# A two-block RWKV / state-space kernel: small products padded to the full array, two heads in turn, fewer changes of array shape

## The chip, the cores and the metric

One core of a Trainium2 chip runs the whole program as one launch. The metric is the device time of that launch in microseconds. Each program was timed in several runs; the median counts. A profile is one further execution, with a span (first to last instruction) and its own time.

## The reference

One sequence of 256 positions, width 2048, float32, through two blocks. The first block has an RWKV-7 time mix (16 heads of 64), a sparse attention with a learned index (16 heads), gates, and a product-key feed-forward with 16384 experts. The second block has a Mamba-2 mixer (64 heads of 64, state 128, 8 groups) and a sliding-window attention. Three parts matter here:

```
# RWKV, per head, for every position t
sa = S @ (-kk_t);  S = S * w_t + sa (kk_t a_t)^T + v_t k_t^T;  y_t = S @ r_t
w_log = -softplus(-(w0 + tanh(zw) @ w_decay_up)) - 0.5
a = sigmoid(a0 + za @ w_icl_up);  g = sigmoid(zg) @ w_gate_up
# Mamba-2, chunks of 128
y_diag = einsum("bgcqs,bgrcqs,bcsgrp->bcqgrp", C B^T, decay_in, x)
y_off  = einsum("bcqgn,bcgrpn,bgrcq->bcqgrp", C, start_states, exp(da_cum))
```

## The kernel before

Large projections run in `K.gemm` (lines 204 and 206): weights come in as float32, ScalarE rounds them to a high part `hi`, VectorE subtracts to get `lo`, and TensorE adds `x*hi` (512 columns) and `x*lo` (256 columns) into one of six large PSUM banks named `g`. The small products work on float32 operands and take one of two small PSUM banks that `k.bank(name)` hands out in turn: `psS`, `psY`, `psQ`, `psA`, `psy` are names of such banks. In the trace a float32 product is two matmul records, here called passes; a transpose or a `g` product is one.

**RWKV** (`Rwkv.pair`, eight pairs of heads, three pairs in flight through `weave`, while a projection's `g` products are put in between by the framework's scheduler). Head 0 of a pair lies on partitions 0 to 63, head 1 on 64 to 127, time is cut in four chunks of 64 (`tt`, `cc`). What the change touches:

- `psA` (lines 464 to 466): the low-rank products for `a` and the gate `g`, with 64, 128 and 32 rows of the array in use.
- `psS` (line 550): the products between chunk vectors, 64 rows each, all four of head 0 into one bank, then all four of head 1 into the other. Five VectorE instructions (lines 554 to 556) read each bank.
- `psQ` (line 642): the state that enters a chunk, times `At`, 64 of 128 output columns in use, three times per pair.
- `psY` (lines 662 and 664): the output. Per chunk two 64-column products (one for each head) and, where a state enters, one of full shape.

**Mamba** (`Mamba.group`, eight groups, as the side generator of a projection). Per half of a group (four heads, `hh`), two units `u` each fill a bank `psy`: four products with 64 output columns that need the decay matrix `M` (line 1528), then two full ones that don't (lines 1530, 1533), then the reads.

In the notation of the trace, 64\*128 is 64 rows by 128 columns of the array in use. A matmul's instruction carries an array shape: 128\*128 (full), 64\*128 and 32\*128 (rows only in part) or 128\*64 (columns only in part).

Of the kernel before, what the change touches and what calls it, by code (L numbers as in the profile page):

```python
# [14 lines left out]
AF = mybir.ActivationFunctionType  # L15
ALU = mybir.AluOpType
# [4 lines left out]
T = 256  # L21
# [351 lines left out]
class Rwkv:  # L373
# [56 lines left out]
    def lora(self):  # L430
        k, nc, pool = self.k, self.k.nc, self.pool
        th = self.th = pool.tile([65, T], F32, name="th")
        nc.vector.memset(th[64:65, :], 1.0)
        nc.scalar.activation(th[0:64, :], self.z[24][0:64, :], AF.Tanh)
        self.za = self.z[24]
        for z in (self.z[25], self.z[26][0:32]):
            k.sigmoid(z, z)

    WIDTH = 3

    def pair(self, hp):
        k, nc, pool, par, c = self.k, self.k.nc, self.pool, self.par, self.c
        f0 = hp * 128
        col = lambda n: par[n][:, hp:hp + 1]
        W = lambda n, shape, bufs=1, dt=F32, p=pool: p.tile(shape, dt, tag="w_" + n, bufs=bufs, name=n)
        L = lambda n, shape: W(n, shape, self.WIDTH)
        last = self.last
        V, S, P, E = nc.vector, nc.scalar, nc.gpsimd, nc.tensor
        halves = [slice(0, 64), slice(64, 128)]
        le, lt = c["leC"], c["ltC"]  # L450

        r, kr, v = (W(f"z{n}", [128, T]) for n in "rkv")
        for i, t in enumerate((r, kr, v)):
            nc.sync.dma_start(t, self.zd[8 * i + hp])
        wg = W("wg", [128, 2, 128])
        fs = slice(f0, f0 + 128)
        nc.scalar.dma_start(wg[:, 0, :], k.a["w_gate_up"][0, 0:128, fs])
        nc.scalar.dma_start(wg[0:32, 1, :], k.a["w_gate_up"][0, 128:160, fs])
        nc.scalar.dma_start(wg[64:128, 1, :], k.a["w_icl_up"][0, :, fs])
        wd = W("wd", [65, 128], 2)  # L460
        nc.scalar.dma_start(wd[0:64, :], k.a["w_decay_up"][0, :, fs])
        nc.scalar.dma_start(wd[64:65, :], k.a["w0"][:, fs])
        psA = k.bank("psA")
        E.matmul(psA[:, 0:T], lhsT=wg[64:128, 1, :], rhs=self.za[64:128, :], start=True, stop=True)
        E.matmul(psA[:, T:], lhsT=wg[:, 0, :], rhs=self.z[25], start=True, stop=False)
        E.matmul(psA[:, T:], lhsT=wg[0:32, 1, :], rhs=self.z[26][0:32, :], start=False, stop=True)
        av = W("a", [128, T])
        k.sigmoid(av, psA[:, 0:T], self.ha0[:, hp:hp + 1])
        g = L("g", [128, T])
        S.copy(g, psA[:, T:])  # L470
        ps = k.bank("psD")
# [8 lines left out]
        for tt in range(2):  # L480
            for i in range(2):
                E.matmul(psC[:, tt * 256:(tt + 1) * 256], lhsT=s2[:, i, tt * 128:(tt + 1) * 128], rhs=self.tri,
                         start=(i == 0), stop=(i == 1))
# [29 lines left out]
        Ah, Rh = AR[:, 0], AR[:, 1]  # L513
        BK = W("BK", [128, 2, 4, 64])
# [8 lines left out]
        two = lambda ap: ap.rearrange("p q t -> p (q t)")  # L523
# [3 lines left out]
        for tt in range(2):  # L527
            ps = k.bank("psR")
# [13 lines left out]
        MR = L("MR", [128, 2, 2, 2, 64])  # L542
        for i, hs in enumerate(halves):
            P.memset(LB[hs, :, halves[1 - i]], 0.0)
            P.memset(LK[hs, :, halves[i]], 0.0)
        for h in range(2):
            ps = k.bank("psS").rearrange("p (a c b t) -> p a c b t", a=2, c=2, b=2)
            for tt in range(2):
                for cc in range(2):
                    E.matmul(ps[:, tt, cc], lhsT=two(BK[halves[h], tt, 2 * cc:2 * cc + 2]),  # L550
                             rhs=AR[halves[h], :, tt, halves[cc]], start=True, stop=True)
            for i, hs in enumerate(halves):
                m = lt[hs, None, :].to_broadcast([64, 2, 64])
                V.tensor_tensor(LB[hs, 2 * h:2 * h + 2, hs], ps[hs, :, i, 0], m, op=ALU.mult)
                V.tensor_tensor(LK[hs, 2 * h:2 * h + 2, halves[1 - i]], ps[hs, :, 1 - i, 0], m, op=ALU.mult)
            V.tensor_tensor(MR[:, h], ps[:, :, :, 1], le[:, None, None, :].to_broadcast([128, 2, 2, 64]), op=ALU.mult)
            yield
        psX = k.bank("psX")
        for i in range(4):
            h, tt = divmod(i, 2)  # L560
            E.matmul(psX[:, i * 64:(i + 1) * 64], lhsT=LK[:, i, :], rhs=VS[:, tt, h], start=True, stop=True)
        S.copy(XA[:, :, 0], psX[:, 0:256].rearrange("p (h a v) -> p a h v", h=2, a=2))
        UV = W("UV", [128, 2, 2, 2, 64], 2)
# [10 lines left out]
        ps = k.bank("psT0")  # L574
# [6 lines left out]
        for lv in range(4):  # L581
            ps = k.bank("psU")
# [5 lines left out]
            ps = k.bank("psW")  # L588
# [4 lines left out]
            ps = k.bank("psV")  # L593
# [32 lines left out]
        ps = k.bank("psT1")  # L626
        for tt in range(2):
            E.transpose(ps[:, tt * 128:(tt + 1) * 128], XA[:, tt, 1].rearrange("p h d -> p (h d)"), k.ident)
        At = W("At", [128, 2, 128], 2)
# [3 lines left out]
        y = W("y", [128, T], 2, p=last)  # L633
        Sd = None
        for tt in range(2):
            starts = []
            for cc in range(2):
                cs = halves[cc]
                starts.append(Sd)
                if Sd is not None:  # L640
                    ps = k.bank("psQ")
                    E.matmul(ps[cs, 0:128], lhsT=At[:, tt, cs], rhs=Sd, start=True, stop=True)
                    u = UV[cs, tt, cc]
                    V.tensor_tensor(u, ps[cs, 0:128].rearrange("p (h v) -> p h v", h=2), u, op=ALU.add)
                    yield
                if tt == 1 and cc == 1:
                    break
                ps2 = k.bank("psZ")
                if Sd is not None:
                    E.matmul(ps2[:, 0:128], lhsT=k.ident, rhs=Sd, start=True, stop=False)  # L650
                E.matmul(ps2[:, 0:128], lhsT=ROW[:, tt, cc], rhs=two(UV[:, tt, cc]), start=(Sd is None), stop=True)
                Sn = W("St", [128, 128], 4, p=last)
                P.memset(Sn, 0.0)
                for h, hs in enumerate(halves):
                    S.activation(Sn[hs, hs], ps2[hs, hs], AF.Copy, scale=gC[hs, tt, cc:cc + 1])
                Sd = Sn
                yield
            psY = k.bank("psY")
            for cc, s in enumerate(starts):
                cs = halves[cc]  # L660
                for h, hs in enumerate(halves):
                    E.matmul(psY[hs, cs], lhsT=UV[:, tt, cc, h], rhs=MR[:, h, tt, cc], start=True, stop=(s is None))
                if s is not None:
                    E.matmul(psY[:, cs], lhsT=s, rhs=Rh[:, tt, cs], start=False, stop=True)
            S.copy(y[:, tt * 128:(tt + 1) * 128], psY[:, 0:128])
            yield

        psG = k.bank("psG")
# [706 lines left out]
class Mamba:  # L1375
# [93 lines left out]
    def group(self, g):  # L1469

        k, nc, pool, c = self.k, self.k.nc, self.pool, self.c
        V, S, P, E = nc.vector, nc.scalar, nc.gpsimd, nc.tensor
        W = lambda n, shape, bufs=2, dt=F32: pool.tile(shape, dt, tag="w_" + n, bufs=bufs, name=n)
        B, C = self.xs[32 + g], self.xs[40 + g]
        xs = self.xs[4 * g:4 * g + 4]
        h0 = 8 * g

        xd = W("xd", [128, 2, 8, 64])
        psb = k.bank("psb")
        for ch in range(2):  # L1480
            cs = slice(ch * 128, (ch + 1) * 128)
            ps = k.bank("psx")
# [23 lines left out]
        for hh in range(0, 8, 4):  # L1506
            M = []
            for ch in range(2):
                r4 = W("r4", [128, 2, 4, 128], dt=F32R)
                ps = k.bank("psg")  # L1510
                for i in range(4):
                    h = h0 + hh + i
                    S.activation(r4[:, 0, i], c["le"], AF.Copy, scale=self.dar[:, ch, h:h + 1])
                    (V if i % 2 else P).tensor_scalar(r4[:, 1, i], c["le"], self.dal[:, ch, h:h + 1], None, op0=ALU.mult)
                for i in range(2):
                    E.matmul(ps, lhsT=self.gt, rhs=r4[:, i].rearrange("p h t -> p (h t)"), start=(i == 0), stop=(i == 1))
                m = W("m", [128, 4, 128], 3)
                S.activation(m, ps.rearrange("p (h t) -> p h t", h=4), AF.Exp)
                V.tensor_tensor(m, m, cb[:, ch, None, :].to_broadcast([128, 4, 128]), op=ALU.mult)
                M.append(m)  # L1520
                yield
            for u in range(2):
                j = (hh + 2 * u) // 2
                hA = hh + 2 * u
                ps = k.bank("psy")
                for ch in range(2):
                    for e in range(2):
                        E.matmul(ps[64 * e:64 * e + 64, ch * 128:(ch + 1) * 128], lhsT=xd[:, ch, hA + e, :],
                                 rhs=M[ch][:, 2 * u + e, :], start=True, stop=True)
                E.matmul(ps[:, 256:384], lhsT=st[:, hA * 64:hA * 64 + 128], rhs=C[:, 128:256], start=True, stop=True)  # L1530
                db = W("db", [128, 2, 64])
                P.tensor_copy(db, self.dar[:, 1, h0 + hA:h0 + hA + 2, None].to_broadcast([128, 2, 64]))
                E.matmul(ps[:, 384:512], lhsT=db.rearrange("p e d -> p (e d)"), rhs=c["le"], start=True, stop=True)
                ec = W("ec", [128, 128])
                S.activation(ec, ps[:, 384:512], AF.Exp)
                V.tensor_tensor(ec, ps[:, 256:384], ec, op=ALU.mult)
                x = xs[j]
                V.scalar_tensor_tensor(x, x, self.dcol[:, 4 * g + j:4 * g + j + 1], ps[:, 0:T], op0=ALU.mult, op1=ALU.add)
                P.tensor_tensor(x[:, 128:256], x[:, 128:256], ec, op=ALU.add)
                yield  # L1540

# [525 lines left out]
```

## Time and profile before

| | |
|---|---|
| median of 3 runs | 3754.48 us (3749.0 to 3759.8) |
| the profiled execution's own time | 3757.85 us |
| its span | 3756.1 us |
| granted TensorE clock, mean | 0.992 |
| TensorE busy | 3634.1 us, 97% of the span |
| weight loads / VectorE / ScalarE / GpSimd busy | 80% / 71% / 53% / 35% |

The page's shares of busy time are averages over stages. A table by stretch tells which engine is full in a stage; the list of instructions in order of time gives the start of each group, and the distance between the start of one and of the next is what it costs in the stream. Durations of matmuls overlap and are modelled, so here only starts are compared. `x8` at the end of a row of that list means eight passes in a row.

### The profile page before, as it was taken

Reading aid. Unit: us, or ns where it says so; the run is one execution under the profiler, and the core shown is the slowest. Engines: PE = TensorE matmul, PEld = TensorE weight load, DVE = VectorE, ACT = ScalarE, POOL = GpSimd, SP = SyncE. Lnnn points to the kernel's source line nnn. Section 1 sums busy time; section 2 is a strip of 40 time slices with the busy share of each in tenths; the row PEclk is TensorE's granted clock in tenths of the full one; section 3 lists DMA queues with packets and bytes.
Section 4 is the critical chain, followed back from the end, with each engine's and each line's share of the span. In section 5 each row is a group of like instructions: output and inputs, shape, how many; then the busy total and the mean of one; then the engine's idle time right before and its main releaser. Section 6 shows DMA issues by size and latency. Waiting matters only on the chain.

```text
span 3756.1 us, 56311 instructions
## 1 busy us (share of the span) xinstructions
PE 3634.1 (97%) x19927; PEld 3023.4 (80%) x19927; DVE 2671.5 (71%) x4261; ACT 1985.7 (53%) x3739; POOL 1320.7 (35%) x1322
## 2 busy tenths in 40 slices
PE   9999999999999999998899999999999999989998
PEld 7778878878888888877788888887888887878777
DVE  5776767666688888888644444446899879577776
ACT  5445555545454677766444444445555666444553
POOL 1333223321288777655511111112144443151101
PEclk9999999999999999999999999999999999999999
DMA  7453433568598888878777766665544445545334
GB/s 219 125 165 113 130 107 110 169 225 254 166 204 207 199 212 222 210 180 207 232 236 239 239 231 231 223 197 182 180 151 146 153 134 165 184 150 185 124 113 136
DMA packets 358335, 681.24 MB, mean 181 GB/s; under 512 B 43981, under 2 KB 111477, under 8 KB 354853
## 3 DMA queue, kind: packets, MB, share of 16 engines
q1 hardware_dynamic: 305216, 591.50, 53.9%
q10 hardware_dynamic: 52837, 86.14, 6.9%
q8 instruction: 158, 2.59, 0.3%
q14 instruction: 124, 1.02, 0.1%
HBM read 627.57 MB, written 47.22 MB: 180 GB/s over the span
## 4 chain that ended last, share of the span: by engine, by line
PE 45%; DVE 8%; DMA 2%; issue 2%; ACT 2%; POOL 0%; ACTq 0%; DVEq 0%; SPq 0%; POOLq 0%
PE g L204 12%; PE g L206 6%; PE gv L1238 5%; PE gv L1237 5%; PE gv L1236 5%; DVE tr L1176 2%; PE dv L1236 2%; PE dv L1237 2%; PE dv L1238 2%; DVE lo L141 2%; DVE oh L1152 1%; ACT hi L139 1%; PE psl L1825 1%; PE g L228 1%; PE pso L1852 1%
## 5 line engine op out<-in xcount | busy, mean ns | idle before, releaser
L141 DVE TENSOR_TENSOR lo<-raw,hi 128x1024 fp32r<-128x1024 f32 (+3 forms) x856 | 1047.1, 1226 | 697.7 <-ACT hi L139 677.8
L139 ACT CAST hi<-raw 128x1024 fp32r<-128x1024 f32 (+3 forms) x858 | 867.5, 1014 | 979.7 <-PE g L204 345.4
L204 PE MATMUL g<-x,hi 128*128 128x512 f32 x3040 | 1089.3, 400 | 13.2 <-DVE x L1646 9.0
L206 PE MATMUL g<-x,lo 128*128 128x256 f32 x3040 | 842.8, 288 | 11.4 <-DVE lo L141 11.2
L1195 PE MATMUL gu<-x,hi 128*128 128x512 f32 x2048 | 733.7, 398 | 4.1 <-ACT hi L139 4.1
L141 POOL TENSOR_TENSOR lo<-tr,hi 128x512 fp32r<-128x512 f32 x429 | 591.5, 1408 | 262.0 <-ACT hi L139 182.3
L204 PEld LDWEIGHTS g<-x,hi 128*128 128x128 f32 x3040 | 568.2, 189 | 135.6 <-issue 19.6
L206 PEld LDWEIGHTS g<-x,lo 128*128 128x128 f32 x3040 | 574.6, 189 | 46.2 <-DVE lo L141 19.5
L1196 PE MATMUL gu<-x,lo 128*128 128x256 f32 x2048 | 581.6, 284 | 13.2 <-POOL lo L141 9.7
L1195 PEld LDWEIGHTS gu<-x,hi 128*128 128x128 f32 x2048 | 386.9, 189 | 91.1 <-ACT hi L139 5.4
L1196 PEld LDWEIGHTS gu<-x,lo 128*128 128x128 f32 x2048 | 387.7, 189 | 22.2 <-POOL lo L141 16.9
L1176 DVE STREAM_TRANSPOSE tr<-raw 128x1024 f32<-128x1024 f32 x256 | 309.1, 1231 | 88.9 <-POOL lo L141 47.8
L139 ACT CAST hi<-tr 128x512 fp32r<-128x512 f32 x512 | 289.4, 615 | 65.0 <-PE gu L1195 37.0
L141 POOL TENSOR_TENSOR g<-scr,g 128x512 fp32r<-128x512 f32 x64 | 112.2, 1754 | 574.4 <-ACT g L139 574.4
L1238 PE MATMUL gv<-hi,g 128*128 128x512 f32 x756 | 299.7, 396 | 0.0
L1237 PE MATMUL gv<-lo,g 128*128 128x512 f32 x756 | 299.7, 396 | 0.0
L1236 PE MATMUL gv<-hi,g 128*128 128x512 f32 x756 | 238.4, 396 | 0.0
L1204 ACT ACTIVATE act<-act 128x256 f32<-128x256 f32 x128 | 53.4, 417 | 242.2 <-DVE act L240 224.7
L204 PE MATMUL g<-y2m,hi 128*128 128x512 f32 x512 | 173.6, 395 | 0.0
L1238 PEld LDWEIGHTS gv<-hi,g 128*128 128x128 f32 x756 | 142.4, 188 | 34.7
L1237 PEld LDWEIGHTS gv<-lo,g 128*128 128x128 f32 x756 | 142.4, 188 | 34.7
L1236 PEld LDWEIGHTS gv<-hi,g 128*128 128x128 f32 x756 | 142.4, 188 | 34.7
(595 smaller groups left out, 5912.1 us busy)
## 6 DMA issues: line engine op xcount, KB each, us to landing
raw<-in_peer_u_dram SPq DMA_DIRECT2D x512, 256.0 KB
raw<-in_peer_v_dram SPq DMA_DIRECT2D x256, 512.0 KB
raw<-in_a_w_in_dram SPq DMA_DIRECT2D x160, 512.0 KB
raw<-in_w_in_dram SPq DMA_DIRECT2D x136, 512.0 KB
raw<-in_b_w_in_dram SPq DMA_DIRECT2D x64, 512.0 KB
raw<-in_a_w_out_dram SPq DMA_DIRECT2D x48, 512.0 KB
raw<-in_w_out_dram SPq DMA_DIRECT2D x32, 512.0 KB
raw<-in_w_peer_query_dram SPq DMA_DIRECT2D x32, 512.0 KB
```

The costliest lines, as they stand in the source:

```text
L139: ins = nc.scalar.copy(hi, x) if heng == "act" else nc.vector.tensor_copy(hi, x)
L141: return ins, eng.tensor_tensor(lo, x, hi.bitcast(F32), op=ALU.subtract)
L204: nc.tensor.matmul(ps[f], lhsT=hi[:, k, f * 128:(f + 1) * 128], rhs=x2[:, q, :], start=(q == 0), stop=False)
L206: nc.tensor.matmul(ps[f][:, 0:T], lhsT=lo[:, k, f * 128:(f + 1) * 128], rhs=x2[:, q, 0:T], start=False, stop=(q == nk - 1))
L228: nc.tensor.matmul(ps[tt], lhsT=x, rhs=lo[:, k, 0:n], start=False, stop=False)
L1176: st["t"] = nc.vector.transpose(tr.rearrange("p b (u j) -> p u b j", u=2), raw[:, 2 * u:2 * u + 2].rearrange("p u (b j) -> p u b j", j=32))
L1195: nc.tensor.matmul(ps, lhsT=hi[:, j], rhs=self.hn2[:, q, :], start=(q == 0), stop=False)
L1196: st["m"] = nc.tensor.matmul(ps[:, 0:T], lhsT=lo[:, j], rhs=self.hn2[:, q, 0:T], start=False, stop=(q == KT - 1))
L1204: nc.scalar.activation(o, o, AF.Gelu)
L1236: nc.tensor.matmul(p, lhsT=x, rhs=hi, start=first, stop=False)
L1237: nc.tensor.matmul(p, lhsT=x, rhs=lo, start=False, stop=False)
L1238: nc.tensor.matmul(p, lhsT=g2[:, T + tt * 128:T + tt * 128 + 128], rhs=hi, start=False, stop=last)
```

## The change

- **psA**: both low-rank operands are laid out over 128 partitions, with zeros written in the unused ones (three memsets on GpSimd once, one of 32 partitions per pair), so all three products use the full shape.
- **psS**: both heads' banks are taken at once, and the loops are turned so that the two heads come in turn.
- **psQ**: all 128 columns of `At` are used instead of 64; only the needed half is read.
- **psY**: the two 64-column products of a chunk become one of 128 columns by 128 columns of both heads; the state's product gets its 64 columns repeated for both heads; the off-diagonal quarters are never read. One ScalarE copy becomes two of half the partitions.
- **psy**: both units' banks are taken at once. The full products of both come first, then all eight 64-column ones, then the reads.

```diff
@@ Rwkv.lora
-        self.za = self.z[24]
         for z in (self.z[25], self.z[26][0:32]):
             k.sigmoid(z, z)
+        nc.gpsimd.memset(self.z[24][0:64], 0.0)
+        for r in (slice(32, 64), slice(64, 128)):
+            nc.gpsimd.memset(self.z[26][r], 0.0)
@@ Rwkv.pair
+        P.memset(wg[32:64, 1, :], 0.0)
...
-        E.matmul(psA[:, 0:T], lhsT=wg[64:128, 1, :], rhs=self.za[64:128, :], start=True, stop=True)
+        E.matmul(psA[:, 0:T], lhsT=wg[:, 1, :], rhs=self.z[24], start=True, stop=True)
         E.matmul(psA[:, T:], lhsT=wg[:, 0, :], rhs=self.z[25], start=True, stop=False)
-        E.matmul(psA[:, T:], lhsT=wg[0:32, 1, :], rhs=self.z[26][0:32, :], start=False, stop=True)
+        E.matmul(psA[:, T:], lhsT=wg[:, 1, :], rhs=self.z[26], start=False, stop=True)
...
-        for h in range(2):
-            ps = k.bank("psS").rearrange("p (a c b t) -> p a c b t", a=2, c=2, b=2)
-            for tt in range(2):
-                for cc in range(2):
-                    E.matmul(ps[:, tt, cc], lhsT=two(BK[halves[h], tt, 2 * cc:2 * cc + 2]),
+        both = [k.bank("psS").rearrange("p (a c b t) -> p a c b t", a=2, c=2, b=2) for _ in range(2)]
+        for tt in range(2):
+            for cc in range(2):
+                for h in range(2):
+                    E.matmul(both[h][:, tt, cc], lhsT=two(BK[halves[h], tt, 2 * cc:2 * cc + 2]),
                              rhs=AR[halves[h], :, tt, halves[cc]], start=True, stop=True)
+        for h, ps in enumerate(both):
...
-                    E.matmul(ps[cs, 0:128], lhsT=At[:, tt, cs], rhs=Sd, start=True, stop=True)
+                    E.matmul(ps[:, 0:128], lhsT=At[:, tt], rhs=Sd, start=True, stop=True)
...
-                for h, hs in enumerate(halves):
-                    E.matmul(psY[hs, cs], lhsT=UV[:, tt, cc, h], rhs=MR[:, h, tt, cc], start=True, stop=(s is None))
+                E.matmul(psY[:, cc], lhsT=two(UV[:, tt, cc]), rhs=MR[:, :, tt, cc], start=True, stop=(s is None))
                 if s is not None:
-                    E.matmul(psY[:, cs], lhsT=s, rhs=Rh[:, tt, cs], start=False, stop=True)
-            S.copy(y[:, tt * 128:(tt + 1) * 128], psY[:, 0:128])
+                    E.matmul(psY[:, cc], lhsT=s, rhs=Rh[:, tt, None, halves[cc]].to_broadcast([128, 2, 64]), start=False,
+                             stop=True)
+            for h, hs in enumerate(halves):
+                S.copy(y[hs, tt * 128:(tt + 1) * 128].rearrange("p (c t) -> p c t", c=2), psY[hs, 0:2, h])
@@ Mamba.group
+            ps = [k.bank("psy") for _ in range(2)]
+            for u in range(2):
+                hA = hh + 2 * u
+                db = W("db", [128, 2, 64])
+                P.tensor_copy(db, self.dar[:, 1, h0 + hA:h0 + hA + 2, None].to_broadcast([128, 2, 64]))
+                E.matmul(ps[u][:, 256:384], lhsT=st[:, hA * 64:hA * 64 + 128], rhs=C[:, 128:256], start=True, stop=True)
+                E.matmul(ps[u][:, 384:512], lhsT=db.rearrange("p e d -> p (e d)"), rhs=c["le"], start=True, stop=True)
+            for u in range(2):
+                for ch in range(2):
+                    for e in range(2):
+                        E.matmul(ps[u][64 * e:64 * e + 64, ch * 128:(ch + 1) * 128], lhsT=xd[:, ch, hh + 2 * u + e, :],
+                                 rhs=M[ch][:, 2 * u + e, :], start=True, stop=True)
```

The scheduler makes TensorE's order anew. In its order of instructions before, the array's shape changes 473 times; now, 305 times. Away from the two stages the order of TensorE is the same.

TensorE in the RWKV stage before, in the fourth pair (`psS_3391` is head 0's bank, `psS_3415` head 1's; `psY` and `psW` belong to the pairs ahead):

```order
L584 MATMUL psU_3377<-TT_3164,LB_3062 128x64 x4
L204 MATMUL g_5935<-o2b_89,hi_5941 128x512
L550 MATMUL psS_3391<-AR_3323,BK_3324 128x128 x4
L662 MATMUL psY_3401<-MR_2777,UV_2821 64x64 x2
L664 MATMUL psY_3401<-AR_2727,St_3275 128x64
L662 MATMUL psY_3401<-MR_2777,UV_2821 64x64 x2
L664 MATMUL psY_3401<-AR_2727,St_3354 128x64
L206 MATMUL g_5935<-o2b_89,lo_5942 128x256
L204 MATMUL g_5935<-o2b_89,hi_5941 128x512
L206 MATMUL g_5935<-o2b_89,lo_5942 128x256
L590 MATMUL psW_3409<-U_3382,Q_3156 128x64 x4
```

Head 1's four `psS` products stand three rows further down. Now, in the same place:

```order
L589 MATMUL psU_3381<-TT_3168,LB_3067 128x64 x4
L554 MATMUL psS_3395<-AR_3327,BK_3328 128x128 x3
L554 MATMUL psS_3396<-AR_3327,BK_3328 128x128 x3
L554 MATMUL psS_3395<-AR_3327,BK_3328 128x128
L554 MATMUL psS_3396<-AR_3327,BK_3328 128x128
L206 MATMUL g_5929<-o2b_89,lo_5957 128x256
L204 MATMUL g_5929<-o2b_89,hi_5956 128x512
L206 MATMUL g_5929<-o2b_89,lo_5957 128x256
```

Both heads stand together, in turn; then nine `g` products (three are shown), then `psY`, now four products of 128x128. Of the eight pairs six have `psS` in one visit to the shape that had two, the first had one already, and one pair still has two.

TensorE in the Mamba stage before, one half of a group (`psy_26154` and `psy_26168` are the two units):

```order
L1528 MATMUL psy_26154<-m_26116,xd_26034 64x128 x2
L1528 MATMUL psy_26168<-m_26116,xd_26034 64x128 x2
L1528 MATMUL psy_26154<-m_26131,xd_26034 64x128 x2
L1530 MATMUL psy_26154<-xs41_25113,st_26079 128x128
L1533 MATMUL psy_26154<-const_ssd_24312,db_26160 128x128
L1528 MATMUL psy_26168<-m_26131,xd_26034 64x128 x2
L1530 MATMUL psy_26168<-xs41_25113,st_26079 128x128
L1533 MATMUL psy_26168<-const_ssd_24312,db_26174 128x128
```

And now, the end of the same half (the four full products stand ahead, among `g` products):

```order
L204 MATMUL g_26352<-x2_78,hi_26651 128x512
L1538 MATMUL psy_26149<-m_26111,xd_26029 64x128 x2
L1538 MATMUL psy_26150<-m_26111,xd_26029 64x128 x2
L1538 MATMUL psy_26149<-m_26126,xd_26029 64x128 x2
L1538 MATMUL psy_26150<-m_26126,xd_26029 64x128 x2
L206 MATMUL g_26352<-x2_78,lo_26652 128x256
```

Two visits to the 64-column shape became one here. Over the sixteen halves the visits for `psy` fall from 46 to 28.

## Rows read from the trace of the kernel before

**Rows 1.** The page, busy time by engine.

```profile
PE 3634.1 (97%) x19927; PEld 3023.4 (80%) x19927; DVE 2671.5 (71%) x4261; ACT 1985.7 (53%) x3739; POOL 1320.7 (35%) x1322
```

**Rows 2.** Busy us by stretch: RWKV, Mamba; length, engines, clock, DMA share, GB/s.

```profile
240.00:720.00 480.00, 464.50 (x2959) 387.53 (x2958) 342.43 (x656) 259.79 (x543) 142.06 (x225) 0.99 0.39 123
2700.00:3080.00 380.00, 380.00 (x2291) 317.85 (x2290) 323.71 (x590) 222.75 (x445) 167.65 (x225) 1.00 0.46 147
```

**Rows 3.** PE in order of time around one psQ; start us, length us, engine, line.

```profile
419.14 0.39 PE L204 MATMUL g<-o2b,hi 128*128 128x512 f32 x1
419.37 0.28 PE L206 MATMUL g<-o2b,lo 128*128 128x256 f32 x1
419.49 0.40 PE L204 MATMUL g<-o2b,hi 128*128 128x512 f32 x1
419.82 0.43 PE L642 MATMUL psQ<-St,At 128*64 128x128 f32 x2
420.18 0.39 PE L206 MATMUL g<-o2b,lo 128*128 128x256 f32 x1
420.41 0.39 PE L204 MATMUL g<-o2b,hi 128*128 128x512 f32 x1
```

**Rows 4.** The same view, the fourth pair's psS, then psY and psW.

```profile
421.57 0.47 PE L204 MATMUL g<-o2b,hi 128*128 128x512 f32 x1
421.97 1.16 PE L550 MATMUL psS<-AR,BK 64*128 64x128 f32 x8
423.06 0.34 PE L662 MATMUL psY<-MR,UV 128*64 128x64 f32 x4
423.32 0.43 PE L664 MATMUL psY<-AR,St 128*128 128x64 f32 x2
...
424.20 0.37 PE L206 MATMUL g<-o2b,lo 128*128 128x256 f32 x1
...
424.75 1.10 PE L590 MATMUL psW<-U,Q 128*128 128x64 f32 x8
425.66 0.48 PE L204 MATMUL g<-o2b,hi 128*128 128x512 f32 x1
```

**Rows 5.** The same view, the first pair, where both heads' psS ran together.

```profile
274.97 1.72 PE L550 MATMUL psS<-AR,BK 64*128 64x128 f32 x16 [0.15 <-ACT VS L535]
276.62 0.50 PE L204 MATMUL g<-x,hi 128*128 128x512 f32 x1
```

**Rows 6.** The same view, psA of one pair.

```profile
445.80 0.70 PE L464 MATMUL psA<-z,wg 64*128 64x256 f32 x2
...
447.68 0.71 PE L473 MATMUL psD<-wd,th 65*128 65x128 f32 x4
```

**Rows 7.** The same view, full-shape passes of 256 columns.

```profile
101.72 1.03 PE L748 MATMUL psN<-csq,const_f 128*128 128x256 f32 x4
102.39 0.58 PE L204 MATMUL g<-x,hi 128*128 128x512 f32 x1
```

**Rows 8.** The same view: psy in the Mamba stage, twelve passes together, four alone.

```profile
2775.05 0.88 PE L1528 MATMUL psy<-m,xd 128*64 128x128 f32 x12
2775.86 0.49 PE L1530 MATMUL psy<-xs,st 128*128 128x128 f32 x2
...
2970.08 0.28 PE L206 MATMUL g<-x,lo 128*128 128x256 f32 x1
2970.29 0.44 PE L1528 MATMUL psy<-m,xd 128*64 128x128 f32 x4
2970.66 0.49 PE L204 MATMUL g<-x,hi 128*128 128x512 f32 x1
```

**Rows 9.** By line: a copy, a memset, the longest read of psS; ns min/median/max, start us.

```profile
L665 ACT COPY y<-psY x16: 265/265/266, 352.6 to 700.5; 128x128 f32<-128x128 f32 x16
...
L545 POOL MEMSET M<- x16: 304/306/309, 236.1 to 597.1; 64x256 f32 x16
...
L556 DVE TENSOR_TENSOR MR<-psS,const_rw x16: 423/425/427, 277.2 to 645.3; 128x256 f32<-128x256 f32 x16
```

More of the change, by code (lines that the diff above doesn't have):

```diff
@@ L657, in pair @@
                 yield
-            psY = k.bank("psY")
+            psY = k.bank("psY").rearrange("p (c h t) -> p c h t", c=4, h=2)
             for cc, s in enumerate(starts):
-                cs = halves[cc]
-                for h, hs in enumerate(halves):
-                    E.matmul(psY[hs, cs], lhsT=UV[:, tt, cc, h], rhs=MR[:, h, tt, cc], start=True, stop=(s is None))
+                E.matmul(psY[:, cc], lhsT=two(UV[:, tt, cc]), rhs=MR[:, :, tt, cc], start=True, stop=(s is None))
                 if s is not None:
-                    E.matmul(psY[:, cs], lhsT=s, rhs=Rh[:, tt, cs], start=False, stop=True)
-            S.copy(y[:, tt * 128:(tt + 1) * 128], psY[:, 0:128])
+                    E.matmul(psY[:, cc], lhsT=s, rhs=Rh[:, tt, None, halves[cc]].to_broadcast([128, 2, 64]), start=False,
+                             stop=True)
+            for h, hs in enumerate(halves):
+                S.copy(y[hs, tt * 128:(tt + 1) * 128].rearrange("p (c t) -> p c t", c=2), psY[hs, 0:2, h])
             yield
@@ L1521, in group @@
                 yield
+            ps = [k.bank("psy") for _ in range(2)]
[10 more added lines that the diff above has]
+                                 rhs=M[ch][:, 2 * u + e, :], start=True, stop=True)
             for u in range(2):
                 j = (hh + 2 * u) // 2
[L1524 to L1533, printed above, removed]
                 ec = W("ec", [128, 128])
-                S.activation(ec, ps[:, 384:512], AF.Exp)
-                V.tensor_tensor(ec, ps[:, 256:384], ec, op=ALU.mult)
+                S.activation(ec, ps[u][:, 384:512], AF.Exp)
+                V.tensor_tensor(ec, ps[u][:, 256:384], ec, op=ALU.mult)
                 x = xs[j]
-                V.scalar_tensor_tensor(x, x, self.dcol[:, 4 * g + j:4 * g + j + 1], ps[:, 0:T], op0=ALU.mult, op1=ALU.add)
+                V.scalar_tensor_tensor(x, x, self.dcol[:, 4 * g + j:4 * g + j + 1], ps[u][:, 0:T], op0=ALU.mult, op1=ALU.add)
                 P.tensor_tensor(x[:, 128:256], x[:, 128:256], ec, op=ALU.add)
```

## The prediction

> **What bounds the kernel now.** I read the page first, for the engine that is full: TensorE is busy for 97% of the span, VectorE for 71% [rows 1]. That is an average, so the table by stretch comes next, for the two stages that the change touches. In the RWKV stretch (240 to 720 us) TensorE is busy for 464.5 of 480 us and VectorE for 342; in the Mamba stretch (2700 to 3080 us) TensorE is busy for all 380 us and VectorE for 324 [rows 2]. In both the granted clock is 0.99 or 1.00, so the 2.4 GHz level holds nearly throughout. Projection products fill the holes that the small products leave; whatever TensorE is spared there lets the next projection product start earlier, until another engine is late. Then I read TensorE's list in order of time, for the distance from start to start.
>
> In full shape the stream is regular: a `hi` product to the next `lo` takes 0.23 us (419.14 to 419.37), a `lo` to the next `hi` 0.12 us [rows 3]. A full-shape float32 pass of up to 128 columns takes about 0.11 us (psW: 0.91 us for eight) [rows 4], one of 256 columns 0.22 us (psN: 0.67 us to the start of the next group, three steps and a short hand-over) [rows 7].
>
> Where the shape changes, the steps are longer. Before psQ the step is 0.33 instead of 0.23, psQ's two passes take 0.36, and the product after it needs 0.23 instead of 0.12 [rows 3]. The visit costs 0.10 + 0.36 + 0.11 = 0.57 us of stream. Two full passes would cost 2 x 0.11 = 0.22. So a visit to another shape carries about 0.35 us that is not columns; the clock is full, no row names an engine that was waited for, and it comes back at every visit. That is what the change goes after.
>
> **The change part by part.** The sum is made in the profiled execution, against its own 3757.85 us.
>
> - psQ, 24 of them (three per pair): each goes from 0.57 to 0.22 us. 24 x 0.35 = 8.4 us.
> - psA, eight pairs: the group takes 1.88 us (445.80 to 447.68) [rows 6], and I add the 0.10 of an entry. It becomes six passes of 0.22, 1.32 us. 8 x 0.66 = 5.3 us.
> - psY: the second block of a pair takes 1.14 us (423.06 to 424.20) [rows 4] and becomes four products, eight passes of 0.11, 0.88 us. 8 x 0.26 = 2.1 us. The repeated 64 columns are free at this price, since psW's passes have 64 columns and take 0.11 as well. The first block loses two visits' edges but its six passes get no shorter; I take nothing for it.
> - psS: eight passes in the half-row shape take 1.09 us (421.97 to 423.06) [rows 4], 0.21 over 8 x 0.11, and the entry 0.10. Six pairs lose one visit: 6 x 0.31 = 1.9 us. Where both heads ran in one visit, 16 passes took 1.65 us (274.97 to 276.62) [rows 5], 0.32 less than 16 x 0.11 + 0.21: passes of the two heads ran side by side where head 0 meets head 1. Now the heads meet at three places in most pairs. I take what one meeting gave, 6 x 0.32 = 1.9 us. The bounds are nothing and eight steps (0.88) in each of six, 5.3 us.
> - psy: four passes alone take 0.37 us (2970.29 to 2970.66), twelve 0.81 us (2775.05 to 2775.86), so eight more cost 0.44, 0.11 a pair of passes. Of the 0.37, 0.15 is the visit's. The entry adds 0.09 (0.21 instead of 0.12 from 2970.08) [rows 8], the exit 0.11 as at psQ. 18 visits fewer x 0.35 = 6.3 us.
>
> Sum: 8.4 + 5.3 + 2.1 + 3.8 + 6.3 = 25.9 us, 19.6 in the RWKV stage and 6.3 in Mamba.
>
> What is added. The memsets are of 0.31 us or less [rows 9], eleven on a GpSimd that is busy for 142 of 480 us; that covers them. Only the first psA waits for one more, behind the tanh that reads `z[24]`: at most 0.3 us, once. Sixteen more ScalarE copies cost at most 0.27 us each [rows 9], 4.2 us on an engine with 220 us to spare in the stretch; they lie between psY and a pair's normalisation, and the next pairs' products and the projection run meanwhile. Without that cover it would be the 4.2 us. DMA traffic hardly changes. psS now holds both small banks until VectorE has read them; that is the third rival's.
>
> What of the 25.9 us arrives. TensorE idles 15.5 us of the RWKV stretch already [rows 2], so the pairs' chain through ScalarE and VectorE is late now and then, and it will be late more often when TensorE comes sooner. In Mamba VectorE is at 85%. I take four fifths, 21 us: 3757.85 - 21 = 3737. The median of the runs lies 3.4 us under the profiled execution, so the runs should show **3733 us**, 0.6% less. About 0.3% (11 us, 3743) is what a measurement of this kernel can tell from no change.
>
> **What speaks against padding.** psY's two 64-column products, one for each head, took 0.26 us together for four passes, edge included [rows 4], where two full passes take 0.22: narrow products do run side by side, and two heads in one padded product keep that gain. The Trainium skill, TensorEngine Tiling, "Theoretical Speedup", gives up to twice the speed for a side of 64 or less; padding gives that up. By that rule alone psQ and psA would gain nothing from the wider shape. The rows decide: psQ and psA have nothing beside them and pay 0.36 for two passes, not 0.11.
>
> Passes of the two heads of psS ran side by side at one meeting, for 0.32 us [rows 5]. The Trainium skill, TensorE: Matmul & The Clock Gate, "What overlaps and what doesn't", says that matmuls of different row groups run at once; by that rule the loop turned to alternate heads would reach the upper bound, 5.3 instead of 1.9 us, and the time would be about 3730. The instruction order alternates strictly in only two pairs; I keep the one meeting.
>
> **The rivals.**
>
> 1. *The other engines take it.* The gain stays in TensorE's stream, and its idle time grows by most of it: the pairs' chain sets the RWKV stage, VectorE the Mamba stage. For it: 15.5 us of idle time and 85% of VectorE [rows 2]. Against it: 97% and 100% of TensorE, and a projection that supplies work at any time. A third arrives: 25.9 / 3 = 8.6 us, 3746 us.
> 2. *The excess belongs to float32 products in the stream, not to the shape.* Then padding removes nothing. Against it: psW, eight full passes between projection products, shows 0.11 a pass [rows 4]. 3754 us, or a little more with the copies.
> 3. *Slower, by the two small banks.* psS takes both at once, and psY or whatever comes next needs one. VectorE reads each head's bank with five instructions, each up to 0.43 us [rows 9]: up to 2.1 us a head. Behind psS stand nine projection products, five of 0.12 and four of 0.23, 1.5 us. If VectorE starts at once, head 0's bank is free 0.6 us after them. It decides when VectorE is busy elsewhere: 25.9 + 11.3 us of new waits, 4.7 us for each of eight pairs, would make it slower by over 0.3%, so the reads would have to start 4 us late in every pair. At 5 us a pair it is 3754 + 40 - 26 = 3768 us. Against it: VectorE is free for 138 of 480 us.
>
> **How the numbers follow.** The forecast gets 0.71, the first rival 0.18, the second 0.04, the slower one 0.07. Faster by over 0.3% is the forecast and a fifth of rival 1: 0.75. Within 0.3%: the rest of rival 1 and rival 2, 0.18. Slower by over 0.3%: 0.07. The range: if all arrives and psS reaches its bound, 25.9 + 3.4 = 29 us, 3725, and 4 us for the scatter of the runs give 3721 below. Above, it takes in rival 1 with 2 us of scatter, 3748. That leaves out rivals 2 and 3 and some scatter.
>
> **What would show it.** psQ with two steps of 0.11 and 0.23 and 0.12 around it; psA from start to psD 1.3 us; one psS visit of 16 passes between 1.1 and 2.0 us; 28 visits for psy; the RWKV stretch shorter by some 15 us, Mamba by 5, the others by nothing. It would be wrong if the padded passes took more than 0.11 (0.22 for psA), or if TensorE's idle time in 240 to 720 us grew by more than 8 us, above all ahead of psY and psW, waiting for VectorE's reads of psS.

## The result and the profile after

| | before | after |
|---|---|---|
| median of 6 runs each | 3756.51 us (3749.0 to 3759.8) | 3737.42 us (3735.42 to 3740.74) |
| ratio of the runs after to the runs before, 95% interval | | 0.9943 (0.9933 to 0.9954) |
| the profiled execution's own time | 3757.85 us | 3738.01 us |
| its span | 3756.1 us | 3736.2 us |

The change made the kernel faster by 0.57% by that ratio; the medians lie 19.1 us apart, which is 0.51%. The time forecast was 3733 us.

The page after, busy time by engine (compare [rows 1]):

```profile
PE 3607.4 (97%) x19863; PEld 3022.5 (81%) x19863; DVE 2673.2 (72%) x4261; ACT 1996.4 (53%) x3761; POOL 1330.4 (36%) x1333
```

TensorE lost 26.7 us of busy time and only 64 passes. The other engines have the same work within 11 us. By stretch (the columns of [rows 2]):

```profile
240.00:720.00 480.00, 463.64 (x2989) 401.63 (x2988) 352.19 (x670) 275.44 (x574) 150.89 (x241) 0.99 0.42 132
2700.00:3080.00 380.00, 378.14 (x2309) 321.45 (x2308) 331.83 (x598) 231.37 (x462) 175.90 (x226) 1.00 0.47 150
```

TensorE idles 16.4 of 480 us in the RWKV stretch, where it idled 15.5. The engine that was full is still full, with more work done in the same stretch.

Where the time came from is read off the same products in both traces. The view of one tile's instructions ends each row with the start of the first and of the last one. Before (psA opens the RWKV stage, `m` is projected after it, `gu` is the expert stage, psx opens Mamba, psn closes it, `g<-x` ends with the last attention):

```profile
L464 PE MATMUL psA<-z,wg x16: 376/428/480, 249.2 to 606.5; 64*128 64x256 f32 x16
L204 PE MATMUL g<-m,hi x256: 388/390/497, 824.3 to 922.4; 128*128 128x512 f32 x128
L1195 PE MATMUL gu<-x,hi x2048: 389/394/632, 1018.8 to 1869.2; 128*128 128x512 f32 x187
L1484 PE MATMUL psx<-const_f,hh x32: 270/272/273, 2737.6 to 2872.5; 128*128 128x128 f32 x32
L1563 PE MATMUL psn<-nacc,const_f x16: 377/379/446, 3070.4 to 3172.5; 128*128 128x256 f32 x16
L204 PE MATMUL g<-x,hi x3040: 387/394/803, 12.2 to 3620.4; 128*128 128x512 f32 x190
```

After, the same view:

```profile
L468 PE MATMUL psA<-z,wg x16: 378/379/483, 249.3 to 597.5; 128*128 128x256 f32 x16
L204 PE MATMUL g<-m,hi x256: 387/390/497, 804.9 to 902.6; 128*128 128x512 f32 x128
L1201 PE MATMUL gu<-x,hi x2048: 389/394/795, 998.9 to 1854.0; 128*128 128x512 f32 x187
L1490 PE MATMUL psx<-const_f,hh x32: 270/272/273, 2721.6 to 2852.3; 128*128 128x128 f32 x32
L1571 PE MATMUL psn<-nacc,const_f x16: 377/378/379, 3041.8 to 3151.9; 128*128 128x256 f32 x16
L204 PE MATMUL g<-x,hi x3040: 387/394/799, 12.0 to 3601.2; 128*128 128x512 f32 x190
```

The lead is nothing where RWKV begins (249.2 and 249.3), 19.4 us at the first `m` product, 19.9 at the first `gu`, 15.2 at the last `gu`, 16.0 at the first psx, 20.6 at the last psn and 19.2 at the last `hi` product of `g<-x`. So RWKV gave 19.5 us, Mamba 4.6, and the expert stage, whose code is the same, took 4.7 back. The second profile of the changed kernel (from the last session) gives 18.9 for RWKV and 6.5 for Mamba; there the expert stage took back 0.8, and what follows Mamba 3.0. So the two stages that were changed gain in both profiles, while the 4.7 are one profile's.

Not all of RWKV's part is the change's. Before, TensorE ran for some microseconds at the lower clock level around the last psA, and around the same products after it did not. The stretches before and after (the columns of [rows 2]):

```profile
604.00:614.00 10.00, 9.27 (x33) 6.42 (x33) 3.04 (x7) 5.80 (x13) 0.73 (x1) 0.66 0.11 20
595.00:605.00 10.00, 9.91 (x63) 8.70 (x63) 8.15 (x18) 8.51 (x20) 5.44 (x7) 1.00 0.42 133
```

Ten microseconds at a granted clock of 0.66 are 3.4 us of clock (an estimate from that row), so about 16 of RWKV's 19.5 us are the change's.

The PE list in order of time shows how the visits look now. psQ (compare [rows 3]), psS and psY (compare [rows 4]), and psA (compare [rows 6]):

```profile
417.88 0.39 PE L204 MATMUL g<-o2b,hi 128*128 128x512 f32 x1
418.11 0.46 PE L647 MATMUL psQ<-St,At 128*128 128x128 f32 x2
418.33 0.36 PE L206 MATMUL g<-o2b,lo 128*128 128x256 f32 x1
418.53 0.39 PE L204 MATMUL g<-o2b,hi 128*128 128x512 f32 x1
...
419.94 1.69 PE L554 MATMUL psS<-AR,BK 64*128 64x128 f32 x16
421.56 0.38 PE L206 MATMUL g<-o2b,lo 128*128 128x256 f32 x1
...
423.21 0.38 PE L666 MATMUL psY<-MR,UV 128*128 128x128 f32 x2
...
424.02 0.48 PE L204 MATMUL g<-o2b,hi 128*128 128x512 f32 x1
...
441.41 0.59 PE L468 MATMUL psA<-z,wg 128*128 128x256 f32 x2
...
442.70 0.61 PE L477 MATMUL psD<-wd,th 65*128 65x128 f32 x4
```

psQ takes 0.22 us (418.11 to 418.33) and is entered at the regular 0.23; only the `lo` product behind it still needs 0.20 in place of 0.12. psS has sixteen passes in 1.62 us, where one head's eight took 1.09. psY takes 0.81 us (423.21 to 424.02), psA 1.29 (441.41 to 442.70).

### The profile page after: what moved, and what is told of

Its sections match the earlier page's. It is cut to its first block, busy times and chain, and to the rows that moved or that the text cites. A ratio compares the mean times of both kernels' runs of the same rounds, so it can differ in the third digit from the quotient of the medians.

```text
span 3736.2 us, 56246 instructions
## 1 busy us (share of the span) xinstructions
PE 3607.4 (97%) x19863; PEld 3022.5 (81%) x19863; DVE 2673.2 (72%) x4261; ACT 1996.4 (53%) x3761; POOL 1330.4 (36%) x1333
## 4 chain that ended last, share of the span: by engine, by line
PE 45%; DVE 8%; DMA 2%; issue 2%; ACT 1%; POOL 0%; ACTq 0%; DVEq 0%; SPq 0%; POOLq 0%
PE g L204 12%; PE g L206 7%; PE gv L1243 5%; PE gv L1244 5%; PE gv L1242 5%; DVE tr L1182 2%; PE dv L1244 2%; PE dv L1242 2%; PE dv L1243 2%; DVE lo L141 2%; DVE oh L1158 1%; ACT hi L139 1%; PE g L228 1%; PE g L227 1%; PE psl L1833 1%
## 5 line engine op out<-in xcount | busy, mean ns | idle before, releaser
L1202 PEld LDWEIGHTS gu<-x,lo 128*128 128x128 f32 x2048 | 386.4, 189 | 25.0 <-POOL lo L141 19.8
```

Of the source, the lines that this page charges most:

```text
L1202: st["m"] = nc.tensor.matmul(ps[:, 0:T], lhsT=lo[:, j], rhs=self.hn2[:, q, 0:T], start=False, stop=(q == KT - 1))
```

## The experiments

Twelve runs (eleven programs, psY alone twice) were made in three sessions, each beside runs of the kernel before, so ratios to it are compared. The changed kernel itself ran again only in the last session; where a run of the second is compared with it, that is across sessions. Stream sums of a tile are worked out from the PE list in one way throughout: from the start of each group to the start of the next product, plus what the steps into it and behind it exceed the regular 0.23, 0.12 or 0.11 us, added over all groups.

**Each part alone**, on the kernel before. psA's edit:

```diff
...
-        E.matmul(psA[:, 0:T], lhsT=wg[64:128, 1, :], rhs=self.za[64:128, :], start=True, stop=True)
+        E.matmul(psA[:, 0:T], lhsT=wg[:, 1, :], rhs=self.z[24], start=True, stop=True)
...
```

> The kernel before with psA alone padded to the full shape. Theory (each visit to another array shape costs about 0.35 us of TensorE's stream, and the stream sets the time in this stage): the group from psA to psD takes 1.3 us instead of 1.88 in every pair, 5.3 us less in the stream, 4 to 5 us less by the end of the RWKV stage, no other stage moves; 3752 us. Rival 1 (other engines take the gain): the group gets shorter, but the stage ends only 1 to 2 us earlier. Rival 2 (the excess belongs to float32 products): the group keeps 1.88 us, no change.

psQ's:

```diff
-                    E.matmul(ps[cs, 0:128], lhsT=At[:, tt, cs], rhs=Sd, start=True, stop=True)
+                    E.matmul(ps[:, 0:128], lhsT=At[:, tt], rhs=Sd, start=True, stop=True)
```

> The kernel before with psQ alone widened to 128 columns. Theory: 24 visits fewer, psQ's two passes 0.22 instead of 0.36 us and the products around it back at 0.23 and 0.12; 8.4 us less in the stream, 6 to 8 us less by the end of the RWKV stage; 3749 us. Rival 1: 2 to 3 us. Rival 2: no change, psQ keeps 0.36.

psS's, both heads in one visit:

```diff
-        for h in range(2):
-            ps = k.bank("psS").rearrange("p (a c b t) -> p a c b t", a=2, c=2, b=2)
-            for tt in range(2):
-                for cc in range(2):
-                    E.matmul(ps[:, tt, cc], lhsT=two(BK[halves[h], tt, 2 * cc:2 * cc + 2]),
+        both = [k.bank("psS").rearrange("p (a c b t) -> p a c b t", a=2, c=2, b=2) for _ in range(2)]
+        for tt in range(2):
+            for cc in range(2):
+                for h in range(2):
+                    E.matmul(both[h][:, tt, cc], lhsT=two(BK[halves[h], tt, 2 * cc:2 * cc + 2]),
...
```

> The kernel before with psS alone: both heads' banks taken at once, heads in turn. Theory: six visits fewer and passes of the two heads side by side where they meet: 3.8 us less in the stream (7 us at most), 3 us less by the end of the stage; 3753 us, hardly to be told from before by the time. The rival with the two banks held: TensorE waits ahead of psY or psW for VectorE's reads of psS and the stage ends later than before, by up to 10 us.

psY's:

```diff
...
-                    E.matmul(psY[hs, cs], lhsT=UV[:, tt, cc, h], rhs=MR[:, h, tt, cc], start=True, stop=(s is None))
+                E.matmul(psY[:, cc], lhsT=two(UV[:, tt, cc]), rhs=MR[:, :, tt, cc], start=True, stop=(s is None))
...
```

> The kernel before with psY alone in full shape. Theory: the second block of a pair 0.89 instead of 1.14 us, 2.1 us less in the stream, 2 us less by the end of the RWKV stage; 3754 us, no change by the time. Rival 2, or padding that costs what it computes: the repeated columns and the unread quarters make psY's blocks longer than 1.14 us.

psy's, where the full-shape products now stand ahead of both units' half-shape ones:

```diff
...
+                E.matmul(ps[u][:, 256:384], lhsT=st[:, hA * 64:hA * 64 + 128], rhs=C[:, 128:256], start=True, stop=True)
...
+            for u in range(2):
...
-                E.matmul(ps[:, 256:384], lhsT=st[:, hA * 64:hA * 64 + 128], rhs=C[:, 128:256], start=True, stop=True)
...
```

> The kernel before with the Mamba part alone. Theory: 18 visits fewer at 0.35, 6.3 us less in the Mamba stage (2700 to 3080 us), nothing in the RWKV stage; 3751 us. Rival 1 (VectorE, 85% busy, sets the stage): TensorE's stream gets shorter but the stage ends at most 2 us earlier.

| part | stream sum before, after | drop | the sum's term | alone: ratio (95%) |
|---|---|---|---|---|
| psQ | 13.8, 8.4 | 5.4 | 8.4 | 0.9979 (0.997 to 0.9987) |
| psA with psD | 21.8, 14.3 | 7.5 | 5.3 | 0.9981 (0.9972 to 0.999) |
| psY | 17.2, 13.7 | 3.5 | 2.1 | 1.0015 (1.0007 to 1.0024) |
| psS | 19.1, 15.5 | 3.6 | 3.8 | 0.9987 (0.9979 to 0.9996) |
| psy | 44.8, 38.8 | 6.0 | 6.3 | 0.9979 (0.9969 to 0.9988) |
| together | | 26.0 | 25.9 | 0.9943 (0.9933 to 0.9954) |

Four parts pay alone: psQ 8 us, psA 7, psS 5 and psy 8 by their ratios, at the least 4.9, 3.8, 1.5 and 4.5 by the intervals. The first rival had allowed psQ 2 to 3, psA 1 to 2 and psy 2, so it falls for these three. For psY the expectation missed: no change was forecast, and it was slower. The five ratios differ from one by -0.59% in sum, the whole by -0.57%: they add up, psY's loss included. psY's products lost time in the stream and yet the kernel was slower; that asked for more.

**psY once more, and the change without psY.** The first is the same kernel again, the second the changed kernel with psY's lines of before put back.

> The kernel before with psY's products alone full size, once more. If the first result (1.0015) was this program's and not that session's, 1.0015 again; if it was scatter between sessions, 0.9995, as its groups of products lose 2 us.

> The changed kernel with psY's products as they were before (64 x 64 and 128 x 64), the rest kept. Theory (each part gives the whole what its own groups of products lose; psY alone came out slower only because the filler products between the small ones were recorded in another order and met other waits): the psY groups are about 2 us longer in the trace, and the time is 0.9943 + 0.0005, so 0.995. Rival (psY's new form costs by itself, by its two ACT copies in place of one, on which the next St waits): the time is 5 us shorter than the changed kernel's, 0.993, and ACT's St is waited for less.

psY alone gave 1.0026 (1.0017 to 1.0036): slower again, so it belongs to this program. Without psY the change gave 0.9954 (0.994 to 0.9967), beside 0.9951 (0.9938 to 0.9965) for the whole change in the same session. The rival, that psY's form is slow by itself and its removal gains 5 us, would be 0.9938 beside that 0.9951 and falls, if narrowly. In the whole change psY is worth nothing that can be measured: its 2 us, which the theory had forecast, lie within the intervals too.

> The changed kernel once more, beside the runs it is compared with. Both theories: 0.9943 of the kernel before, within 0.001.

Two places in the traces show where psY alone loses. The first is in the RWKV stage. The waits of TensorE between 460 and 520 us, second run of psY alone:

```profile
PE psU L584 <- ACT St L655: 1.5, 1, 1.5
```

The PE list at that place:

```profile
499.84 1.10 PE L584 MATMUL psU<-TT,LB 128*128 128x64 f32 x8 [1.52 <-ACT St L655]
...
501.40 0.78 PE L464 MATMUL psA<-z,wg 64*128 64x256 f32 x2
502.11 1.22 PE L465 MATMUL psA<-z,wg 128*128 128x256 f32 x2
503.26 1.22 PE L466 MATMUL psA<-z,wg 32*128 32x256 f32 x2
504.41 1.22 PE L473 MATMUL psD<-wd,th 65*128 65x128 f32 x4
```

And the stretch around it (the columns of [rows 2]):

```profile
500.00:510.00 10.00, 10.00 (x40) 7.13 (x40) 2.24 (x7) 3.26 (x7) 0.73 (x1) 0.66 0.35 122
```

TensorE waited 1.5 us for ScalarE's copies of the state, and behind the wait psA's pairs of passes start 1.15 us apart (502.11 to 503.26), where the kernel before takes 0.63 (a third of the 1.88 in [rows 6]): the granted clock of the ten microseconds is 0.66, so part of them ran at the 1.2 GHz level. The first run of psY alone has the same wait and the same stretch there; the kernel before has neither at that pair, and its projection products stand in other places between the small ones. Across the place (485 to 545 us of the kernel before) the same projection products fall back by 3.5 us in both runs.

The second place is the expert stage. TensorE's largest sum of waits there (total, times, longest; whole span), in the changed kernel:

```profile
PE psg L1161 <- ACT oh L1156: 25.3, 31, 3.2
```

and in the change without psY:

```profile
PE psg L1161 <- ACT oh L1156: 24.3, 32, 1.2
```

The longest single one of these waits is 3.0 to 3.6 us in seven of the eight profiles with the wide psY (1.4 in the eighth) and 1.2 or 1.3 in all six without. Behind it stands the weights' transfer: in the changed kernel VectorE waits 4.3 us for it with a transpose, and ScalarE 6.6 us for a small tile that VectorE computes next. Across the place the `gu` products fall back by 3.6 us in both runs of psY alone and by 3.4 in the changed kernel, by 1.4 without psY. Over the whole stage the same split shows: from the first `gu` product to the last it takes 851.2 to 856.4 us (mean 854.5) in the eight profiles with the wide psY and 848.2 to 852.6 (mean 850.4) in the six without. The two places, 7 us, less the 2.6 that psY's own products save there, make 4 to 5 of the 6 to 10 us. Why that transfer is later with the wide psY stays open: no code of that stage was changed, and no run separates it.

**psQ full size but in two.** On the changed kernel:

```diff
-                    E.matmul(ps[:, 0:128], lhsT=At[:, tt], rhs=Sd, start=True, stop=True)
+                    for hs in halves:
+                        E.matmul(ps[hs, 0:128], lhsT=At[:, tt, hs], rhs=Sd, start=True, stop=True)
```

> The changed kernel with each full psQ product split into two of 64 columns each, first and second half: same operands, same columns, same result, only the array shape differs. Theory (the shape change costs): 24 visits come back, and four passes that run in pairs take about 0.4 us; the stream gets 24 x 0.35 = 8 us longer, 3745 us. Rival 2 (float32 products, not the shape, are dear): the same number of columns in the same place, at most 24 x 0.05 = 1 us longer, 3738 us.

It took 0.9941 (0.9925 to 0.9957): the time does not tell it from the changed kernel, and the 8 us longer that the theory forecast (a ratio of about 0.9964) did not come. The PE list does tell the two apart:

```profile
457.19 0.39 PE L204 MATMUL g<-o2b,hi 128*128 128x512 f32 x1
457.51 0.44 PE L648 MATMUL psQ<-St,At 128*64 128x128 f32 x4
457.88 0.38 PE L206 MATMUL g<-o2b,lo 128*128 128x256 f32 x1
458.10 1.00 PE L595 MATMUL psW<-U,Q 128*128 128x64 f32 x8
```

Entry 0.32, four passes 0.37, exit 0.22: the visit of the kernel before is back, with twice the passes in the same 0.37 us. The stream sum of psQ rises from 8.4 to 13.9 us. With the same data and the same number of output columns, the narrow shape brings the excess back, and not the number of passes, since two of them took 0.36 before; so the second rival falls, by this list and not by the time. Why the 5.5 us do not show in the time stays open: 0.9943 + 0.0015 lies at the upper end of the interval. In the profile the RWKV stage does end later (its first `m` product leads the kernel before by 13.6 us, in the changed kernel's two profiles by 19.4 and 18.2), but it also has a stretch at the lower clock that those lack, at 495 us. The long wait of the expert stage is missing (1.4 in place of 3.2 us), yet that stage is no shorter: 854.6 us from the first to the last `gu`, against 855.1 and 851.2.

**psS head by head.** One visit as in the change, but all of head 0 ahead of head 1:

```diff
-        for tt in range(2):
-            for cc in range(2):
-                for h in range(2):
+        for h in range(2):
+            for tt in range(2):
+                for cc in range(2):
```

> The changed kernel with the psS loops back in the old order, head 0's four products and then head 1's, but both banks taken at once as in the change. It tells what of the psS term is the one visit and what is the heads in turn. Theory: one meeting of the heads, 16 passes in about 1.65 us against 1.62 with the heads in turn as scheduled; no change in time (under 1 us). Rival (heads in turn matters): 1.9 to 2.0 us for the group, 3 us longer in all, 3740 us.

0.9953 (0.9938 to 0.9968): not told apart from the whole change. Its psS in the PE list:

```profile
423.09 1.71 PE L554 MATMUL psS<-AR,BK 64*128 64x128 f32 x16
424.73 0.50 PE L204 MATMUL g<-o2b,hi 128*128 128x512 f32 x1
```

1.64 us against 1.62 in the changed kernel, so the loop's order looks worthless. It is not: the changed kernel's own recorded order hardly alternates. In five of its eight pairs it has three products of head 0, three of head 1 and one of each; in one pair, four and four with a projection product between them; in the first pair, two and two and then in turn (1.65 us). Only the second pair alternates strictly, where the prediction had counted two such pairs, and it takes 1.43 us:

```profile
316.38 1.50 PE L554 MATMUL psS<-AR,BK 64*128 64x128 f32 x16
317.81 0.39 PE L206 MATMUL g<-x,lo 128*128 128x256 f32 x1
```

The last pair of the kernel with psS alone alternates strictly too, and its sixteen passes take 1.09 us, no longer than eight of one head:

```profile
637.68 1.16 PE L550 MATMUL psS<-AR,BK 64*128 64x128 f32 x16
638.77 0.39 PE L206 MATMUL g<-x,lo 128*128 128x256 f32 x1
```

Two more strictly alternating visits, one in the change without psY (527.22) and one in the kernel with psQ in two (578.27), take 1.09 us as well. So the two heads' passes can run wholly side by side, 0.53 us a visit below what most visits take; the change gets half of that overlap. The 1.43 us of the second pair hold a wait: head 1's first product is released by ScalarE's copies out of a small bank, which end at 316.67 in the changed kernel:

```profile
316.13 0.54 ACT L539 COPY VS<-psR 64x128 f32<-64x128 f32 x2
```

Head 1's first pass starts at 316.73, 0.34 us behind head 0's, and 1.43 - 0.34 = 1.09. In the kernel with psS alone the same copies had ended 0.7 us ahead of the visit.

**The same for the attentions.** Of the 305 changes of shape left after the change, most are the attentions'. attn_out gives the output products full-size operands, with the neighbouring head's values (at the edges of the last attention's tile, zeros) beside those needed:

```diff
...
-                    E.matmul(ps[hs, j * 128:(j + 1) * 128], lhsT=self.vr[:, s, kv * 64:kv * 64 + 64], rhs=pT[:, j, s],
+                    E.matmul(ps[:, j * 128:(j + 1) * 128], lhsT=self.vr[:, s, o0:o0 + 128], rhs=pT[:, j, s],
...
```

> The changed kernel with the same step taken further, in both attentions: the product of probabilities and values, 64 output columns until now, gets 128 (the neighbouring head's values beside it) and only the needed half is read. Shape changes in the instruction order fall from 305 to 224. Theory: 40 visits fewer at 0.35 us, 14 us less in the stream, 11 to 14 us less in time, 3725 us. Rival 1 (softmax on VectorE and ScalarE sets the attention stages): 3 to 5 us. Rival 2: no change.

attn_all pads the keys too, with memsets and, in the first attention, two ScalarE copies in place of one for each key tile (three temporaries also move to shared buffers):

```diff
...
-                E.matmul(pv[:, j], lhsT=self.q[hs, h // 2, tt * 128:(tt + 1) * 128], rhs=self.kd[hs, kv, 0:nk],
+                E.matmul(pv[:, j], lhsT=self.q[:, h // 2, tt * 128:(tt + 1) * 128], rhs=self.kd[:, hq % 2, kv, 0:nk],
...
```

> The changed kernel with both attentions' small products in full shape: outputs as in attn_out, scores against keys padded with zeros too. Changes of array shape fall from 305 to 98. Theory (what the groups of products lose arrives): attn_out's groups lost 11.7 us in its trace and the score products should lose 0.25 us at each of some 60 visits, 15 us more, so 3757 - 19 - 27 = 3711 where the kernel before takes 3757 (0.988). Rival (part of it is taken by waits in the attention's chain, as attn_out's total of -5 us suggests): 3725 (0.9916).

attn_out took 0.9927 (0.9911 to 0.9944). That is about 6 us below the changed kernel's 0.9943 from another session, and nearer its first rival (3 to 5 us) than its theory (11 to 14); its interval does not exclude no gain. attn_all took 0.99 (0.9885 to 0.9915): 3721.28 us beside 3740.74 for the changed kernel in that session. attn_all beats both kernels, by 1.0% and 0.5%. Its gain of 19 us lies between the theory's 27 and the rival's 13. The two attentions tell why. The stretches 125 to 245 us (first attention) and 3460 to 3640 us (last) of the changed kernel:

```profile
125.00:245.00 120.00, 116.63 (x615) 87.98 (x615) 88.60 (x175) 61.94 (x142) 36.74 (x61) 1.00 0.47 148
3460.00:3640.00 180.00, 178.91 (x956) 135.98 (x957) 129.21 (x273) 93.98 (x229) 17.02 (x30) 1.00 0.36 115
```

and of attn_all:

```profile
125.00:245.00 120.00, 108.59 (x613) 88.45 (x612) 86.44 (x174) 62.31 (x143) 39.74 (x61) 0.99 0.48 147
3460.00:3640.00 180.00, 179.06 (x1069) 150.57 (x1068) 144.18 (x315) 105.16 (x261) 20.81 (x34) 1.00 0.39 128
```

In the last attention TensorE stays full and gets through 1069 passes in place of 956: the gain arrives. In the first it does 613 in place of 615 and idles 11.4 us in place of 3.4: the eight microseconds saved became idle time. The wait there, psP for VectorE's softmax (`bm`), is 3.1 us in the changed kernel:

```profile
PE psP L840 <- DVE bm L835: 3.1, 6, 0.8
```

and 9.8 in attn_all, so 6.7 of the eight are this wait:

```profile
PE psP L843 <- DVE bm L838: 9.8, 10, 3.1
```

That is the prediction's first rival, at a place that this change did not touch.

## Why the prediction was right

- *What bounds the kernel.* Right. TensorE is at 97% after as before, its idle time in the RWKV stretch grew by 0.9 us where 8 would have refuted it, and RWKV gave 19.5 us (about 16 without the clock at 606 us), Mamba 4.6, where 15 and 5 had been said.
- *psQ, 8.4 us.* Too high: 5.4. The visit before was read rightly (0.56 in the median of the 24, 0.57 said). The mis-sized term is what stays: a visit still costs 8.4 / 24 = 0.35 us in the mean (0.28 in the median) where 0.22 was said. Waits are one part: the steps into the groups exceed the regular ones by 2.4 us in sum (1.0 in the kernel with psQ alone, whose sum falls further, to 6.6). The step behind is the other: where a projection product follows, as it does at half of the 24, it does not fall back to the regular one (0.20 where 0.12 was said). That step was never the shape's. In the kernel before, the `lo` product behind a small float32 product of full shape takes 0.20 too:

```profile
497.51 0.49 PE L651 MATMUL psZ<-UV,ROW 128*128 128x128 f32 x2
497.76 0.36 PE L206 MATMUL g<-x,lo 128*128 128x256 f32 x1
497.96 0.39 PE L204 MATMUL g<-x,hi 128*128 128x512 f32 x1
```

  So 0.08 of the 0.35 us that the prediction gave to the shape belong to the small float32 product, as the second rival would have it. What the shape cost is nearer 0.2 to 0.3: 0.57 less 0.35 in the changed kernel, 0.57 less 6.6 / 24 with psQ alone.
- *psA, 5.3 us.* 7.5, but 1.6 of it is the pair at 606 us that ran at the lower clock before. The other 5.9 is the term: 1.88 became 1.30 in the median (1.32 said), the entry's 0.09 went, and so did 0.10 of the group's end in psD, which the sum had not counted.
- *psY, 2.1 us.* 3.5 in its own sum and nothing in the time. The expert stage, some 4 us longer in the profiles with the wide psY, took it back; why is open. The block named took 0.81 us in place of 1.14. The ScalarE copies show in one wait of TensorE of 0.3 us (below); the prediction had said that they are covered.
- *psS, 3.8 us.* 3.6 in sum. In the prediction's own terms a visit's overlap is 16 x 0.11 + 0.21 - 1.62 = 0.35 us, where 0.32 had been said. By the rule of the Trainium skill, TensorE: Matmul & The Clock Gate, "Part 3: Packing small matmuls — row/col tiling", products of different row groups run at once (the prediction names a paragraph of that part, which speaks of weight loads). The trace agrees where the recorded order alternates strictly (1.09 us), and shows half of it in most visits (1.62), where that order does not; the prediction's choice between the two, one meeting, rested on that order and was right to 0.03 us.
- *psy, 6.3 us.* 6.0.
- *Padding gives up narrow products that run side by side.* By the Trainium skill, TensorEngine Tiling, "Theoretical Speedup", a side of 64 or less gives up to twice the speed; the trace agrees here, as four narrow passes take the 0.37 us that two took. The visit around them costs more than that: 0.56 us for psQ in narrow products, 0.28 in full ones, in the median.
- *Four fifths arrive.* The size was right (19.8 us between the profiled executions, 21 said), in part by luck. By stage the share comes out: about 16 of 19.6 us in RWKV without the clock, 4.6 of 6.3 in Mamba. But two things that no term held nearly cancel: the 3.4 us that the kernel before lost to the clock at 606 us, and the 4.7 that the expert stage took back in this profile (0.8 in the second).
- *Rivals.* The first (the other engines take it) is refuted here by TensorE's idle time; the second by psQ_split's list; the third, the two small banks, by the waits. One wait of TensorE in the RWKV stretch names VectorE's reads of psS (`MR`), and one ScalarE's copies out of psY (`y`):

```profile
PE psQ L647 <- ACT y L671: 0.3, 1, 0.3
PE psW L595 <- DVE MR L561: 0.2, 1, 0.2
```

## What to carry to other kernels

Where one engine is full and has filler work, count its changes of array shape and read their price in its list, start to start: here 0.23 to 0.33 us a visit by the stream sums (psQ 5.4 / 24, psy 6.0 / 18), so that in psQ one full-size product beats two narrow ones run side by side (0.28 against 0.56 us a visit). Before expecting it in the time, look for the wait that comes next in that stage: the first attention turned its gain into idle time, most of it waiting for VectorE, the last one did not. A part of a few microseconds can be lost to where a recorded order then puts a wait, so judge it by its own steps in the trace and by the whole set, not by one run alone.

## What had not been expected of the hardware

- Passes of the two row halves overlap even head by head, where they meet (1.64 us for sixteen), and wholly in strictly alternating visits where no wait held the second head (1.09 in each of three kernels).
- One wait of 1.5 us was followed by a stretch at a granted clock of 0.66, in which psA's steps nearly doubled (1.15 us a pair of passes, 0.63 before). Such stretches cost some 2 to 3.4 us each (an estimate from their granted clocks), and they come and go: one at 606 us is in the kernel before and not in the changed one, one at 282 us is in one profile of the changed kernel and not in the other. That is the size of the parts that were being measured.
